# A hybrid decoder layer on one core: the last TensorE transposes of h and of the S5 table factor ea replaced by VectorE block transposes and copies through DRAM

## The chip, the cores and the metric

The kernel runs on one core of a Trainium2 chip. The metric is the device time of one execution in microseconds (us). All inputs, products and outputs are float32; the large products are made from float32 numbers split into two parts.

## The reference, cut to what matters

One decoder layer on 256 positions of width 2048. The two FFNs (width 5632) and the input and output projections of the mixer carry nearly all the work. Between the FFNs stands a mixer of two halves: an S5 state-space half (64 groups of 16 channels with 64 complex states) and a chunked gMLP half.

```python
h = h + 0.5 * swiglu(rms_norm(h, norm_ffn1), w1_gate, w1_up, w1_down)
z = rms_norm(h, norm_mix) @ w_in
y_ssm = s5_mixer(z[..., :1024], log_dt, a_re, a_im, b_re, b_im, c_re, c_im, d, w_glu)
y_gmlp = gmlp_mixer(z[..., 1024:2048], z[..., 2048:], norm_v, w_s, b_s)
h = h + concatenate([rms_norm(y_ssm, ...), rms_norm(y_gmlp, ...)]) @ w_out
h = h + 0.5 * swiglu(rms_norm(h, norm_ffn2), w2_gate, w2_up, w2_down)
gate = sigmoid(rms_norm(h, norm_ple) @ w_ple_gate)
h = h + gate * (p @ w_ple_proj)
return rms_norm(h, norm_final)

def swiglu(x, w_gate, w_up, w_down):
    return (silu(x @ w_gate) * (x @ w_up)) @ w_down
```

The S5 half depends on its inputs through tables that are functions of the parameters alone (powers of the complex step `abar`, the input factors `b`, the output factors `c`). The kernel computes these tables while FFN1 runs.

## The kernel before, in words

**The stream.** All products with large weights are one stream of steps. A group is one 512-column output of one weight; its depth is walked in steps of two 128-row slices (K slices). In a step ("tick") TensorE makes 12 matmuls of 512 columns: two slices, two halves `t` of the positions, and three products each. The weight tile `raw` is loaded by DMA on SP's queue (`L114`, 1 MB, four slices, 3 buffers), split by ScalarE (ACT) into `wh` (`L133`) and by VectorE (DVE) into the remainder `wl` (`L134`), each in 4 buffers, so the split of step i+3 is written ahead of the products of step i. The products are `wh` with the high part of the activations (`L147`), `wl` with the high part (`L148`), and `wh` with the low part (`L149`).

**The order.** The instructions stand on every engine in the order in which the Python code emits them; nothing reorders them later, and every engine works through its own row from first to last. After each step the loop adds one to `tick_no` and runs the generators that are due. A generator that yields an integer sleeps for that many ticks; under `paced` it yields costs, and sleeps one tick when their sum passes `self.budget` (0.85 in the table rounds). So `yield 6` decides after which step's instructions the next piece stands.

**h to its transpose.** The next product needs h with its columns on partitions, split in two parts: `hTh` and `hTl`, 16 slices. `h_to_T(n, gcol, flip)` makes slices 4n to 4n+3 from the finished 512-column chunk n of h. With `flip` it uses `flip()`: VectorE transposes 32x32 blocks of h into `tr` (`L367`), POOL's DMA queue stores `tr` to the DRAM buffer `gsc` (`L370`), and four DMA loads (`L373`) bring the blocks back to their partitions; after `yield 6`, ACT scales (`L232`) and copies to `hTh` (`L236`), and VectorE subtracts to `hTl` (`L238`). Without `flip`, TensorE transposes 4 blocks at a time against the identity (`L199`), twice. Chunks 0 to 2 of both FFNs and chunks 0 and 2 of `w_out` use `flip`; chunk 3 of each of these three and chunk 1 of `w_out` use TensorE. The same `flip()` also transposes the gated FFN activations (`gTa`, `gTb`, `L203`, `L204`), 22 times. There is one `tr` and two `gsc`.

**The S5 tables.** `s5_tables` runs in the first 280 us or so, in four rounds of the loop over k (`NQ` is 4). A round makes on VectorE the factor `ea` (two tiles, real and imaginary, 128x512) and others into the table tile `qt`; TensorE transposes `ea` (8 transposes of 128x128) and ACT copies them to `qt[:, 2048:3072]` (`L618`); TensorE makes 32 small products `mps` (`L623`); VectorE adds and copies these (`md`, `L628` to `L632`), and SP copies two blocks of `md` by DMA (`L634`). Then POOL sets the first column of the cosine and sine tables (`L639`, `L640`), and VectorE fills them by doubling:

```python
            g.memset(qc[:, :, 0:1], 1.0)
            g.memset(qs[:, :, 0:1], 0.0)
...
                for o, x, y, op in ((c1, c0, pc, M), (tt, s0, psn, M), (c1, c1, tt, SB),
                                    (s1, s0, pc, M), (tt, c0, psn, M), (s1, s1, tt, AD)):
                    gop(o, x, y, op)
```

In its first pass `c0` is `qc[:, :, 0:2]`, the column set by POOL and the one beside it. `put` stores parts of `qt` to DRAM on SP's queue (`L562`): columns 2048 to 4607 after `md`, columns 0 to 2047 at the end of the round.

Of the kernel before, what the change touches and what calls it, by code (L numbers as in the profile page):

```python
# [7 lines left out]
F32 = mybir.dt.float32  # L8
F32R = mybir.dt.float32r
I32 = mybir.dt.int32  # L10
AF = mybir.ActivationFunctionType
ALU = mybir.AluOpType
# [3 lines left out]
P = 128  # L16
# [5 lines left out]
NW = 512  # L22
# [32 lines left out]
class Layer:  # L55
# [166 lines left out]
        j = self.junk_p.tile([P, NW], F32, tag="junk", name="junk")  # L222
        self.nc.scalar.activation(out=j, in_=src, func=AF.Square, accum_out=acc)

    def h_to_T(self, n, gcol, flip):

        if flip:
            tr = self.flip([self.h[:, t, n * NW:(n + 1) * NW] for t in range(2)])
            yield 6
            for kk in range(4):  # L230
                v = tr.rearrange("p (i t kk u) -> p kk (i t) u", i=4, t=2, kk=4)[:, kk]
                self.nc.scalar.activation(out=v, in_=v, func=AF.Copy, scale=self.gcol[:, gcol + 4 * n + kk:gcol + 4 * n + kk + 1])  # L232
            dh, dl = (y[:, 4 * n:4 * n + 4, :].rearrange("p kk (t i u) -> p t kk i u", t=2, i=4) for y in (self.hTh, self.hTl))
            trv = tr.rearrange("p (i t kk u) -> p t kk i u", i=4, t=2, kk=4)
            for t in range(2):
                self.nc.scalar.activation(out=dh[:, t], in_=trv[:, t], func=AF.Copy)  # L236
            for t in range(2):
                self.nc.vector.tensor_tensor(out=dl[:, t], in0=trv[:, t], in1=dh[:, t].bitcast(F32), op=ALU.subtract)  # L238
            return
        for b in range(2):  # L240
            yield 1
            k0 = 4 * n + 2 * b
            ps = self.transposes(
                [self.h[:, t, (k0 + kk) * P:(k0 + kk + 1) * P] for kk in range(2) for t in range(2)])
            self.split_gain2(ps, self.gcol[:, gcol + k0:gcol + k0 + 2], self.hTh[:, k0:k0 + 2], self.hTl[:, k0:k0 + 2])

    def act_hT(self, k, t):
        return self.hTh[:, k, t * P:(t + 1) * P], self.hTl[:, k, t * P:(t + 1) * P]
# [1 line left out]
    def kernel(self):  # L250
        tc, nc, I = self.tc, self.nc, self.i
# [21 lines left out]
        self.stash = dram.tile([2 * NQ, P, BW], F32, name="stash")  # L273
        self.gsc = [dram.tile([P, 4 * 256], F32, name=f"gsc{b}") for b in range(2)]
        self.spot = 0
        self.tr = const.tile([P, 4 * 256], F32, name="tr")
        self.pools, self.cms = {}, {}

        self.plan = []
# [63 lines left out]
    def open_g(self):  # L343
        n = self.KA // 4
        self.gT_a = (self.pools["gta"].tile([P, n, 4 * 256], F32R, name="gTah"),
                     self.pools["gta"].tile([P, n, 4 * 256], F32R, name="gTal"))
        self.open("gs", "gs")

    def open_gb(self):
        self.open("gtb", "gtb")  # L350
# [9 lines left out]
    def flip(self, src):  # L360

        nc, tr = self.nc, self.tr
        trv = tr.rearrange("p (a t kk u) -> p t kk a u", a=4, t=2, kk=4)
        for t in range(2):
            nc.vector.transpose(out=trv[:, t], in_=src[t].rearrange("p (kk a u) -> p kk a u", kk=4, a=4))  # L367
        sc = self.gsc[self.spot]
        self.spot ^= 1
        nc.gpsimd.dma_start(out=sc, in_=tr)  # L370
        sv = sc.rearrange("(i f) (a x) -> a f i x", i=4, a=4)
        for a in range(4):
            nc.gpsimd.dma_start(out=tr[32 * a:32 * a + 32, :].rearrange("f (i x) -> f i x", i=4), in_=sv[a])  # L373
        return tr

    def ffn_groups(self, which):
# [42 lines left out]
        def down_post(n):  # L419
            def post(g):  # L420
                for t in range(2):
                    hs = self.h[:, t, n * NW:(n + 1) * NW]
                    self.nc.vector.scalar_tensor_tensor(
                        out=hs, in0=g.ps[t], scalar=0.5, in1=hs, op0=ALU.mult, op1=ALU.add)
                ssq = self.ssq[1 if which == 1 else 5]
                for t in range(2):
                    self.square(self.h[:, t, n * NW:(n + 1) * NW], ssq[:, n, t:t + 1])
                if n == 3:
                    self.rstd([ssq[:, i, :] for i in range(4)], D, self.r[1 if which == 1 else 4])
                yield from self.h_to_T(n, 16 if which == 1 else 48, n < 3)  # L430
            return post

        for c in range(11):
# [30 lines left out]
    def s5_tables(self):  # L464
# [20 lines left out]
        qt = T("qt", (P, QW))  # L485
# [74 lines left out]
        def put(k, lo, n, wd):  # L560
            for b in range(2):
                nc.sync.dma_start(  # L562
                    out=self.stash[2 * k + b, :, lo // 2:lo // 2 + n * wd].rearrange("p (r x) -> p r x", r=n),
                    in_=qt[:, lo:lo + 2 * n * wd].rearrange("p (r b x) -> p r b x", r=n, b=2)[:, :, b])
        self.budget = 0.85
        for k in range(NQ):
# [47 lines left out]
            yield 1  # L614
            for ri in range(2):
                ef = ea[ri].rearrange("p q t g x -> p (q t g x)")
                ps = self.transposes([ef[:, j * P:(j + 1) * P] for j in range(4)])
                nc.scalar.activation(out=qt[:, 2048 + 512 * ri:2560 + 512 * ri], in_=ps, func=AF.Copy)  # L618
            ps = self.aux_p.tile([P, NW], F32, tag="aux", name="mps")
            for q in range(8):  # L620
                o = ps[64 * (q % 2):64 * (q % 2) + 64, 32 * (q // 2):32 * (q // 2) + 32]
# [10 lines left out]
                v.tensor_copy(out=mt[s, :, 64 * a + 32:64 * a + 64], in_=md[s])  # L632
            for a in range(2):
                nc.sync.dma_start(out=mt[64 * a:64 * a + 32, :, 64 * a:64 * a + 32], in_=md[64 * a + 32:64 * a + 64])  # L634
            put(k, 2048, 5, 256)
            yield 0.6
            qc = qt[:, 0:1024].rearrange("p (q j) -> p q j", q=8)
            qs = qt[:, 1024:2048].rearrange("p (q j) -> p q j", q=8)
# [5 lines left out]
            for m in range(1, 7):  # L644
                n = 1 << m
                pc = C[:, m + 1, q0:q0 + 8].unsqueeze(2).to_broadcast([P, 8, n])
                psn = S[:, m + 1, q0:q0 + 8].unsqueeze(2).to_broadcast([P, 8, n])
                c0, s0, c1, s1 = qc[:, :, 0:n], qs[:, :, 0:n], qc[:, :, n:2 * n], qs[:, :, n:2 * n]
                tt = tmp[:, :, 0:n]
                cost = 0.1 + 0.0084 * n  # L650
                for o, x, y, op in ((c1, c0, pc, M), (tt, s0, psn, M), (c1, c1, tt, SB),
                                    (s1, s0, pc, M), (tt, c0, psn, M), (s1, s1, tt, AD)):
                    gop(o, x, y, op)
                    yield cost
            put(k, 0, 2, 512)


# [134 lines left out]
    def gmlp(self, half):  # L792
# [27 lines left out]
        self.close("gm")  # L820
        self.open("yss", "yss")
        m = self.pools["yss"]
        self.yh = m.tile([P, 8, 256], F32R, name="yh")
        self.yl = m.tile([P, 8, 256], F32R, name="yl")
        self.sg = [m.tile([P, NW], F32, name=f"sg{t}") for t in range(2)]

    def mix_groups(self):
        I, nc = self.i, self.nc
# [67 lines left out]
        def wo_post(n, rr, ssm):  # L896
            def post(g):
                for t in range(2):
                    hs = self.h[:, t, n * NW:(n + 1) * NW]
                    nc.vector.scalar_tensor_tensor(out=hs, in0=g.ps[t], scalar=rr[:, t:t + 1], in1=hs,  # L900
                                                   op0=ALU.mult, op1=ALU.add)
                if not ssm:
                    return
                for t in range(2):
                    self.square(self.h[:, t, n * NW:(n + 1) * NW], self.ssq[4][:, n, t:t + 1])
                if n == 3:
                    self.rstd([self.ssq[4][:, i, :] for i in range(4)], D, self.r[3])
                yield from self.h_to_T(n, 32, n % 2 == 0)
            return post

        def glu_post(n):
# [218 lines left out]
```

## Time and profile before

| what | value |
|---|---|
| median of 3 runs | 1851.15 us (1850.25 to 1851.33) |
| the profiled execution | 1851.49 us, its span 1849.8 us |
| TensorE (PE) busy | 1837.9 us, 99% of the span |
| VectorE (DVE) busy | 1140.3 us, 62% |
| ScalarE (ACT) busy | 854.5 us, 46% |
| GpSimd (POOL) busy | 131.0 us, 7% |
| mean granted TensorE clock | 0.998 of full speed |

The profile is one execution. PE's busy time counts pipelined matmuls whose ends are modelled, so where TensorE loses time is read from the starts of neighbouring matmuls, from its waits, and from the chain of work that ended last.

### The profile page before, as it was taken

The numbers are of one execution on the slowest core, as the hardware profiler recorded it, in microseconds if no ns is written. First come the engines' busy times: TensorE is split into PE (matmuls) and PEld (weight loads), VectorE is DVE, ScalarE is ACT, GpSimd is POOL, SyncE is SP. The second block draws the span as 40 slices with busy tenths as digits, with TensorE's granted clock in tenths as the row PEclk, the third lists the DMA queues.
The fourth block names the chain that finished last, engine by engine and source line by source line (L and its number), as shares of the span: only waits on it lengthen the run. The fifth ranks groups of instructions, "written<-read, shape, count | busy, mean of one in ns | idle before, by whom it ended". The sixth has DMA issues, their size and how long they took to land.

```text
span 1849.8 us, 21900 instructions
## 1 busy us (share of the span) xinstructions
PE 1837.9 (99%) x8512; PEld 1526.8 (83%) x8512; DVE 1140.3 (62%) x1541; ACT 854.5 (46%) x1012; POOL 131.0 (7%) x208
## 2 busy tenths in 40 slices
PE   9999999999999999999999999999999999999998
PEld 7888888888888888888888888888888888888887
DVE  6788886555545554698876555555555555455565
ACT  6444444444444444444446544444444444444454
POOL 1000000000000000022100000000000000000000
PEclk9999999999999999999999999999999999999999
DMA  8677777666656665665546666666666665566553
GB/s 324 223 244 265 235 269 253 217 217 226 220 201 216 216 216 193 225 253 210 188 163 216 213 216 217 217 226 219 222 218 217 216 216 206 204 216 216 190 204 134
DMA packets 72615, 405.10 MB, mean 219 GB/s; under 512 B 10176, under 2 KB 15552, under 8 KB 29888
## 3 DMA queue, kind: packets, MB, share of 16 engines
q1 hardware_dynamic: 62000, 371.67, 56.4%
q0 software_dynamic: 10080, 31.47, 5.8%
q8 instruction: 66, 1.08, 0.2%
q10 hardware_dynamic: 432, 0.57, 0.1%
q14 instruction: 37, 0.30, 0.0%
HBM read 376.28 MB, written 27.26 MB: 218 GB/s over the span
## 4 chain that ended last, share of the span: by engine, by line
PE 98%; DMA 1%; issue 1%; DVE 0%; ACT 0%; SPq 0%; POOLq 0%; POOL 0%; DVEq 0%; ACTq 0%
PE acc L147 32%; PE acc L149 32%; PE acc L148 32%; PE tr L199 1%; PE y L759 1%; DMA raw<-in_w_gate 1%; PE v L712 0%; PE sp L800 0%; PE mps L623 0%; PE y L753 0%; DVE wl L134 0%; ACT wh L133 0%; SPq L296 0%; DVE hg L1052 0%; DVE h L1035 0%
## 5 line engine op out<-in xcount | busy, mean ns | idle before, releaser
L134 DVE TENSOR_TENSOR wl<-raw,wh 128x1024 fp32r<-128x1024 f32 (+1 forms) x649 | 800.9, 1237 | 642.5 <-ACT wh L133 640.7
L133 ACT ACTIVATE wh<-raw 128x1024 fp32r<-128x1024 f32 (+1 forms) x649 | 685.9, 1059 | 824.3 <-PE acc L149 779.6
L147 PE MATMUL acc<-wh,hTh 128*128 128x512 f32 (+1 forms) x1744 | 680.9, 390 | 0.1
L148 PE MATMUL acc<-wl,hTh 128*128 128x512 f32 (+1 forms) x1744 | 678.1, 389 | 1.3 <-DVE wl L134 1.3
L149 PE MATMUL acc<-wh,hTl 128*128 128x512 f32 (+1 forms) x1744 | 678.2, 389 | 0.0
L148 PEld LDWEIGHTS acc<-wl,hTh 128*128 128x128 f32 x1744 | 327.5, 188 | 69.1 <-DVE wl L134 2.1
L149 PEld LDWEIGHTS acc<-wh,hTl 128*128 128x128 f32 x1744 | 327.4, 188 | 68.2
L147 PEld LDWEIGHTS acc<-wh,hTh 128*128 128x128 f32 x1744 | 327.4, 188 | 67.8 <-ACT wh L133 0.5
L147 PE MATMUL acc<-wh,gTah 128*128 128x512 f32 x384 | 149.4, 389 | 0.0
L148 PE MATMUL acc<-wl,gTah 128*128 128x512 f32 x384 | 149.4, 389 | 0.0
L149 PE MATMUL acc<-wh,gTal 128*128 128x512 f32 x384 | 149.4, 389 | 0.0
L147 PE MATMUL acc<-wh,gTbh 128*128 128x512 f32 x320 | 124.5, 389 | 0.0
L148 PE MATMUL acc<-wl,gTbh 128*128 128x512 f32 x320 | 124.5, 389 | 0.0
L149 PE MATMUL acc<-wh,gTbl 128*128 128x512 f32 x320 | 124.5, 389 | 0.0
L370 POOL DMA_DIRECT2D gsc<-tr x30 | 17.0, 568 | 1160.1 <-DVE tr L367 1160.1
L147 PEld LDWEIGHTS acc<-wh,gTah 128*128 128x128 f32 x384 | 72.1, 188 | 15.1
L148 PEld LDWEIGHTS acc<-wl,gTah 128*128 128x128 f32 x384 | 72.1, 188 | 15.0
L149 PEld LDWEIGHTS acc<-wh,gTal 128*128 128x128 f32 x384 | 72.1, 188 | 14.9
L373 POOL DMA_DIRECT2D tr<-gsc x120 | 65.5, 552 | 97.4 <-DMA gsc<-tr 91.2
L147 PEld LDWEIGHTS acc<-wh,gTbh 128*128 128x128 f32 x320 | 60.1, 188 | 12.6
L148 PEld LDWEIGHTS acc<-wl,gTbh 128*128 128x128 f32 x320 | 60.1, 188 | 12.5
L149 PEld LDWEIGHTS acc<-wh,gTbl 128*128 128x128 f32 x320 | 60.1, 188 | 12.4
(233 smaller groups left out, 1061.5 us busy)
## 6 DMA issues: line engine op xcount, KB each, us to landing
raw<-in_w_up SPq DMA_DIRECT2D x88, 1024.0 KB, 5.8
raw<-in_w_down SPq DMA_DIRECT2D x88, 1024.0 KB, 4.8
raw<-in_w_gate SPq DMA_DIRECT2D x86, 1024.0 KB, 4.8
raw<-in_w_in SPq DMA_DIRECT2D x24, 1024.0 KB, 4.8
raw<-in_w_out SPq DMA_DIRECT2D x16, 1024.0 KB, 4.8
raw<-in_w_ple_gate SPq DMA_DIRECT2D x16, 1024.0 KB, 4.9
gsc<-tr POOLq DMA_DIRECT2D x30, 512.0 KB, 3.2
tr<-gsc POOLq DMA_DIRECT2D x120, 128.0 KB, 4.4
```

What stands on the lines that cost most here:

```text
L133: nc.scalar.activation(out=wh[:, 0:nk, :], in_=src, func=AF.Copy)
L134: nc.vector.tensor_tensor(out=wl[:, 0:nk, :], in0=src, in1=wh[:, 0:nk, :].bitcast(F32), op=ALU.subtract)
L147: nc.tensor.matmul(o, ah, wh[:, j, c0:c1], start=first, stop=False)
L148: nc.tensor.matmul(o, ah, wl[:, j, c0:c1], start=False, stop=False)
L149: nc.tensor.matmul(o, al, wh[:, j, c0:c1], start=False, stop=last)
L199: self.nc.tensor.transpose(ps[:, i * P:(i + 1) * P], b, self.ident)
L370: nc.gpsimd.dma_start(out=sc, in_=tr)
L373: nc.gpsimd.dma_start(out=tr[32 * a:32 * a + 32, :].rearrange("f (i x) -> f i x", i=4), in_=sv[a])
L759: nc.tensor.matmul(ps[:, 64 * i:64 * i + 64], R[ri][:, i, :], qt[:, f0:f0 + 64], start=False, stop=(a == 1 and ri == 1))
```

## The change: what it does

1. `h_to_T` always goes through `flip()`. Chunk 3 of FFN1, of `w_out` and of FFN2, and chunk 1 of `w_out` leave TensorE. Chunk 3 sleeps 5 ticks instead of 6.
2. There are two `tr` buffers, used in turn with the two `gsc`; the second lives in pools that are open where it is needed.
3. In a table round the 8 TensorE transposes of `ea` and the two ACT copies are replaced: VectorE transposes 32x32 blocks of both halves straight into `qt`, and POOL's queue stores each half to a DRAM buffer `esc` and loads it back in 16 pieces of 32 partitions, each in runs of 32 elements.
4. The store of columns 2048 to 4607 moves to the end of the round.

```diff
-    def h_to_T(self, n, gcol, flip):
+    def h_to_T(self, n, gcol):
 
-        if flip:
-            tr = self.flip([self.h[:, t, n * NW:(n + 1) * NW] for t in range(2)])
-            yield 6
...
-        for b in range(2):
-            yield 1
-            k0 = 4 * n + 2 * b
-            ps = self.transposes(
-                [self.h[:, t, (k0 + kk) * P:(k0 + kk + 1) * P] for kk in range(2) for t in range(2)])
-            self.split_gain2(ps, self.gcol[:, gcol + k0:gcol + k0 + 2], self.hTh[:, k0:k0 + 2], self.hTl[:, k0:k0 + 2])
+        tr = self.flip([self.h[:, t, n * NW:(n + 1) * NW] for t in range(2)])
+        yield 5 if n == 3 else 6
...
-        self.tr = const.tile([P, 4 * 256], F32, name="tr")
+        self.tr = [const.tile([P, 4 * 256], F32, name="tr"), None]
+        self.esc = [dram.tile([P, NW], F32, name=f"esc{b}") for b in range(2)]
...
+        self.tr[1] = self.pools["gs"].tile([P, 4 * 256], F32, name="tr1")
...
-        nc, tr = self.nc, self.tr
+        nc, tr = self.nc, self.tr[self.spot]
...
                 ef = ea[ri].rearrange("p q t g x -> p (q t g x)")
-                ps = self.transposes([ef[:, j * P:(j + 1) * P] for j in range(4)])
-                nc.scalar.activation(out=qt[:, 2048 + 512 * ri:2560 + 512 * ri], in_=ps, func=AF.Copy)
+                et = qt[:, 2048 + 512 * ri:2560 + 512 * ri]
+                v.transpose(out=et.rearrange("p (a j u) -> p j a u", a=4, j=4),
+                            in_=ef.rearrange("p (j a u) -> p j a u", j=4, a=4))
+                g.dma_start(out=self.esc[ri], in_=et)
+                ev = self.esc[ri].rearrange("(i f) (a j u) -> a f j i u", i=4, a=4, j=4)
+                for a in range(4):
+                    for j in range(4):
+                        g.dma_start(out=qt[32 * a:32 * a + 32, 2048 + 512 * ri + P * j:2176 + 512 * ri + P * j]
+                                    .rearrange("f (i u) -> f i u", i=4), in_=ev[a, :, j])
+                yield 0.8
...
-            put(k, 2048, 5, 256)
...
+            put(k, 2048, 5, 256)
             put(k, 0, 2, 512)
...
+        self.tr[1] = m.tile([P, 4 * 256], F32, name="tr1")
```

Three places of the order of instructions show what moves. In the rows, x16 counts neighbours that read alike, and `[waits ...]` names the semaphores that an instruction waits for (`Pool`, `DVE`, `PE`, `Activation` for an engine, `DMASW` and `DMAHW` for DMAs from POOL's queue and the others).

First POOL's row in the table rounds. Before, two transfers of an FFN activation with the two memsets of round 0 behind them:

```order
L370 DMA gsc_112<-tr 128x1024
L373 DMA tr<-gsc_112 32x4x256 x4
L370 DMA gsc_113<-tr 128x1024
L373 DMA tr<-gsc_113 32x4x256 x4
L639 MEMSET qt 128x8
L640 MEMSET qt 128x8
```

The same place in the changed program:

```order
L364 DMA gsc_112<-tr 128x1024
L367 DMA tr<-gsc_112 32x4x256 x4
L364 DMA gsc_113<-tr_142 128x1024
L367 DMA tr_142<-gsc_113 32x4x256 x4
L614 DMA esc_115<-qt 128x512
L618 DMA qt<-esc_115 32x4x32 x16
L614 DMA esc_116<-qt 128x512
L618 DMA qt<-esc_116 32x4x32 x16
L640 MEMSET qt 128x8
L641 MEMSET qt 128x8
```

In each of the four rounds 34 DMA issues now stand ahead of the two memsets.

Second VectorE's row in round 1, from the second half of the new transpose (`L612`) to the first doubling step, in the changed program:

```order
L612 STREAM_TRANSPOSE qt<-ea_360 128x4x4x32 [waits DMASW3_49,DMASW4_49,DMASW2_49,DMASW1_49]
L134 TENSOR_TENSOR wl<-raw,wh 128x1024 [waits PE_49,Activation_49]
L134 TENSOR_TENSOR wl<-raw,wh 128x1024 [waits DMAHW6_49,Activation_49]
L630 TENSOR_TENSOR md<-dI,mps 128x128 [waits DMAHW1_49,DVE_49,PE_49]
L634 COPY qt<-md 64x4x32 [waits DVE_49]
L634 COPY qt<-md 64x4x32
L642 COPY qt<-C 128x8 [waits DMAHW2_49,DMAHW1_49]
L643 COPY qt<-S 128x8
L552 TENSOR_TENSOR qt<-qt,C 128x8x2 [waits DVE_49,Pool_49]
L552 TENSOR_TENSOR tmp<-qt,S 128x8x2 [waits DVE_49,Pool_49]
L552 TENSOR_TENSOR qt<-qt,tmp 128x8x2 [waits DVE_49]
L134 TENSOR_TENSOR wl<-raw,wh 128x1024 [waits Activation_49]
```

In the program before, the first doubling step carries the same wait, and only the transposes are missing:

```order
L134 TENSOR_TENSOR wl<-raw,wh 128x1024 [waits DMAHW5_49,PE_49,Activation_49]
L628 TENSOR_TENSOR md<-dI,mps 128x128 [waits DMAHW0_49,DMAHW1_49,DVE_49,PE_49]
L632 COPY qt<-md 64x4x32 [waits DVE_49]
L632 COPY qt<-md 64x4x32
L641 COPY qt<-C 128x8 [waits DMAHW1_49,DMAHW0_49]
L642 COPY qt<-S 128x8
L558 TENSOR_TENSOR qt<-qt,C 128x8x2 [waits DVE_49,Pool_49]
```

So the wait for POOL's memset is in both programs; what stands ahead of that memset on POOL is new.

Third ACT's row after the last chunk of FFN1, where the mixer's first group begins. Before, ACT's work on chunk 3 stands one and two steps after the squares of h:

```order
L223 ACTIVATE junk,ssq_102<-h 128x512 x2
L133 ACTIVATE wh<-raw 128x1024
L214 ACTIVATE hTh<-tr,gcol 128x256 x2
L133 ACTIVATE wh<-raw 128x1024
L214 ACTIVATE hTh<-tr,gcol 128x256 x2
L133 ACTIVATE wh<-raw 128x1024 x6
```

In the changed program it stands after five:

```order
L223 ACTIVATE junk,ssq_102<-h 128x512 x2
L133 ACTIVATE wh<-raw 128x1024 x5
L231 ACTIVATE tr<-tr,gcol 128x8x32 x4
L235 ACTIVATE hTh<-tr 128x4x128 x2
L133 ACTIVATE wh<-raw 128x1024 x3
```

Slices 12 to 15 of `hTh` and `hTl`, which these write, are read by TensorE in the seventh step of that group.

## Rows read from the trace of the kernel before

**Rows 1.** The page: busy time by engine, and the granted clock by slice.

```profile
PE 1837.9 (99%) x8512; PEld 1526.8 (83%) x8512; DVE 1140.3 (62%) x1541; ACT 854.5 (46%) x1012; POOL 131.0 (7%) x208
...
PEclk9999999999999999999999999999999999999999
```

**Rows 2.** The waits of PE, whole span: total us, times, longest us.

```profile
PE acc L148 <- DVE wl L134: 1.3, 2, 0.8
```

**Rows 3.** Line L199 on PE: duration ns min/median/max, first and last start.

```profile
L199 PE MATMUL tr<-ident,h x32: 270/272/273, 740.0 to 1747.3; 128*128 128x128 f32 x32
```

**Rows 4.** Timeline of PE after FFN1's last chunk: start us, us, what.

```profile
737.24 0.39 PE L147 MATMUL acc<-wh,hTh 128*128 128x512 f32 x1
...
739.96 0.60 PE L199 MATMUL tr<-ident,h 128*128 128x128 f32 x4
...
743.17 0.60 PE L199 MATMUL tr<-ident,h 128*128 128x128 f32 x4
```

**Rows 5.** The chain that ended last, table round 1: start us, us, what.

```profile
162.31 0.87 PE tr L199 x8
163.19 1.07 PE mps L623 x32
```

**Rows 6.** Timeline of POOL in table rounds: start, us, [idle before <-releaser].

```profile
101.68 0.56 POOL L370 DMA_DIRECT2D gsc<-tr  x1 [38.25 <-DVE tr L367]
105.41 2.18 POOL L373 DMA_DIRECT2D tr<-gsc  x4 [3.17 <-DMA gsc<-tr]
107.58 0.13 POOL L639 MEMSET qt<- 128x8 f32 x1
```

**Rows 7.** Timeline of DVE in table round 1.

```profile
163.00 1.22 DVE L134 TENSOR_TENSOR wl<-raw,wh 128x1024 fp32r<-128x1024 f32 x1
164.85 1.23 DVE L134 TENSOR_TENSOR wl<-raw,wh 128x1024 fp32r<-128x1024 f32 x1 [0.63 <-ACT wh L133]
...
167.07 0.18 DVE L558 TENSOR_TENSOR qt<-qt,C 128x16 f32<-128x16 f32 x1
```

**Rows 8.** DMAs of the tile md: us from issue to landing.

```profile
DMA to landing us min/median/max: 1.8/2.7/3.9
```

**Rows 9.** DMAs of the tile tr, 1010 to 1030 us (contended), issue to landing.

```profile
DMA to landing us min/median/max: 3.2/6.8/8.1
```

**Rows 10.** Timeline of PE at the start: the 32 warm-up matmuls.

```profile
1.44 6.76 PE L288 MATMUL warm<-ident 128*128 128x128 f32 x32 [1.44 <-POOL mhalf L264]
```

**Rows 11.** Timeline of DVE after FFN1's last chunk: the last step of rstd.

```profile
739.38 0.17 DVE L193 TENSOR_SCALAR rs<-rs 128x2 f32<-128x2 f32 x1
```

**Rows 12.** Timeline of one flip of chunk 0 of FFN1, on DVE, POOL and ACT.

```profile
558.63 1.29 DVE L367 STREAM_TRANSPOSE tr<-h 128x512 f32<-128x512 f32 x2
560.22 0.56 POOL L370 DMA_DIRECT2D gsc<-tr  x1 [53.67 <-DVE tr L367]
563.70 2.18 POOL L373 DMA_DIRECT2D tr<-gsc  x4 [2.92 <-DMA gsc<-tr]
572.49 1.69 ACT L232 ACTIVATE tr<-tr,gcol 128x256 f32<-128x256 f32 x4
574.87 1.29 DVE L238 TENSOR_TENSOR hTl<-tr,hTh 128x512 fp32r<-128x512 f32 x2 [1.03 <-ACT hTh L236]
```

**Rows 13.** Timeline of POOL and ACT: two flips for which ACT waited.

```profile
1286.67 0.56 POOL L370 DMA_DIRECT2D gsc<-tr  x1 [37.55 <-DVE tr L367]
1299.40 1.06 ACT L203 ACTIVATE gTah<-tr 128x1024 fp32r<-128x1024 f32 x1 [0.49 <-DMA tr<-gsc]
1330.19 0.56 POOL L370 DMA_DIRECT2D gsc<-tr  x1 [37.58 <-DVE tr L367]
1344.49 1.06 ACT L203 ACTIVATE gTbh<-tr 128x1024 fp32r<-128x1024 f32 x1 [2.06 <-DMA tr<-gsc]
```

**Rows 14.** Waits of ACT for weights, whole span; landing, 166 to 171 us.

```profile
ACT wh L133 <- DMA raw<-in_w_up: 13.9, 5, 7.3
...
stash<-qt SPq DMA_DIRECT2D x2, 640.0 KB, 4.4
```

More of the change, by code (lines that the diff above doesn't have):

```diff
@@ L223, in square @@
         self.nc.scalar.activation(out=j, in_=src, func=AF.Square, accum_out=acc)
-    def h_to_T(self, n, gcol, flip):
-        if flip:
-            tr = self.flip([self.h[:, t, n * NW:(n + 1) * NW] for t in range(2)])
-            yield 6
[L230 to L239, printed above, removed]
-        for b in range(2):
-            yield 1
-            k0 = 4 * n + 2 * b
-            ps = self.transposes(
-                [self.h[:, t, (k0 + kk) * P:(k0 + kk + 1) * P] for kk in range(2) for t in range(2)])
-            self.split_gain2(ps, self.gcol[:, gcol + k0:gcol + k0 + 2], self.hTh[:, k0:k0 + 2], self.hTl[:, k0:k0 + 2])
+    def h_to_T(self, n, gcol):
+        tr = self.flip([self.h[:, t, n * NW:(n + 1) * NW] for t in range(2)])
+        yield 5 if n == 3 else 6
+        for kk in range(4):
+            v = tr.rearrange("p (i t kk u) -> p kk (i t) u", i=4, t=2, kk=4)[:, kk]
+            self.nc.scalar.activation(out=v, in_=v, func=AF.Copy, scale=self.gcol[:, gcol + 4 * n + kk:gcol + 4 * n + kk + 1])
+        dh, dl = (y[:, 4 * n:4 * n + 4, :].rearrange("p kk (t i u) -> p t kk i u", t=2, i=4) for y in (self.hTh, self.hTl))
+        trv = tr.rearrange("p (i t kk u) -> p t kk i u", i=4, t=2, kk=4)
+        for t in range(2):
+            self.nc.scalar.activation(out=dh[:, t], in_=trv[:, t], func=AF.Copy)
+        for t in range(2):
+            self.nc.vector.tensor_tensor(out=dl[:, t], in0=trv[:, t], in1=dh[:, t].bitcast(F32), op=ALU.subtract)
     def act_hT(self, k, t):
@@ L429, in post @@
                     self.rstd([ssq[:, i, :] for i in range(4)], D, self.r[1 if which == 1 else 4])
-                yield from self.h_to_T(n, 16 if which == 1 else 48, n < 3)
+                yield from self.h_to_T(n, 16 if which == 1 else 48)
             return post
@@ L907, in post @@
                     self.rstd([self.ssq[4][:, i, :] for i in range(4)], D, self.r[3])
-                yield from self.h_to_T(n, 32, n % 2 == 0)
+                yield from self.h_to_T(n, 32)
             return post
```

## The prediction

> **What bounds the kernel now.** I read the page first: PE is busy for 1837.9 of 1849.8 us, at a granted clock of nine tenths or more in every slice [rows 1]. Then PE's waits: for the weight split it waited 1.3 us in the whole span, in two waits [rows 2]. So TensorE is fed without a gap, and only its own instruction count sets the time. Anything removed from it is gained one for one; every stall that the change gives it is lost one for one. The other engines have idle time, but it is bounded by a lead: VectorE writes the remainder `wl` three steps ahead of its use, and beyond that TensorE stands. What matters is therefore how long VectorE or ACT, which work through their rows in order, are held at one place.
>
> **What is removed.** The 32 transposes of h [rows 3] stand in eight blocks of four. A step of 12 matmuls took 739.96 - 737.24 = 2.72 us; the step with a block took 743.17 - 739.96 = 3.21 us [rows 4]. That is 0.49 us a block, 3.9 us for eight. In a table round the eight transposes of `ea` take 0.87 us of the chain, and the 32 small products follow at once, as before [rows 5]: 4 x 0.87 = 3.5 us. Together **-7.4 us**. The two ACT copies a round also go; ACT is 46% busy and nothing waits longest for it, so I count nothing.
>
> **What the tables get.** Each half of `ea` is a store on POOL's queue, then 16 loads that read what it wrote. POOL is in order: in round 0 it stored at 101.68, waited for the landing, issued its first load at 105.41, took 2.18 us for four, and the memset followed at 107.58, the moment the last issue was done [rows 6]. So an issue takes 0.545 us, and the memset cannot pass the DMAs. Now 34 issues and two landings stand ahead of it, and the first doubling step of VectorE waits for it. In round 1 of before that step ran at 167.07, five microseconds after TensorE's transposes [rows 5, 7], because the memset had long been done.
>
> Worked out for round 1, from E = 162.31, the end of the step's products [rows 5]:
> VectorE's `wl` ends at 163.00 + 1.22, so the new transposes start at E + 1.9 [rows 7] and take 1.29 as those of h do; POOL starts 0.3 later (558.63 + 1.29 to 560.22) [rows 12]: E + 3.5. From a store to its first load 563.70 - 560.22 = 3.5 us pass [rows 12]; the new store is half as large, I keep 3.5. Sixteen loads are 8.7 us. Twice 12.2 is 24.4; the memset ends at E + 28.0. Three short doubling steps (0.18 each) and the next `wl` (1.23) [rows 7] make E + 29.8. TensorE meanwhile has the small products (1.07) [rows 5], the five steps whose `wl` stands before the wait (13.6), and one matmul (0.23, a twelfth of a step): E + 14.9. It stands for 14.9 us, in four rounds 60 us. In round 3 the finished gate group's two products and their transposes also stand between the wait and the next `wl`; at 1.29 us for the transposes and as much again for the products that is 2.6 more: **+62 us**.
>
> The bounds. Below: VectorE not 1.9 us late at E, and half a microsecond less for each of the two smaller stores, gives 12.0 a round, 48 in all. Above: the program gives POOL's DMAs eight semaphores in turn, so a load waits for the one eight before it. Where a load lands in under 8 x 0.545 = 4.4 us this costs nothing. The 16 KB copies of `md`, in the same 128-byte runs, landed in 2.7 us, 3.9 at most [rows 8]; in a contended stretch the loads of `tr` had a median of 6.8 [rows 9]. With 6.8 a load would be issued every 0.85 us, 4.9 us more a set, 9.8 a round: 101 us in all. I take 0.545, because rows 8 have the same size and runs, and because a standing VectorE frees no weight buffers, so the weight loads pause.
> The Trainium skill ("DMA: Bandwidth & Descriptors", Specifications) says that pieces under 512 B are not moved at line rate, since the engine reads, changes and writes them. By that rule the loads would go towards the far end, and the sum to some 1960 instead of 1920; rows 8 show no such penalty at this size, and no row shows 32 such copies in a queue.
>
> **What the last chunk of h gets.** Its transfer stands after the row statistics: VectorE is done with them at 739.38 + 0.17 [rows 11], so the transposes end at 740.84 and the store starts 0.3 later. Against G = 737.24, the start of the next group [rows 4], that is G + 3.9. Where ACT waited for a transfer, the data was there 1299.40 - 1286.67 = 12.7 us after the store, elsewhere 14.3 [rows 13]. From ACT's start to the end of the last subtraction 574.87 + 1.29 - 572.49 = 3.7 us pass [rows 12]. TensorE uses the last of it in the sixth matmul of the seventh step, 6 x 2.72 + 5 x 0.227 = G + 17.4. So ACT may start at G + 13.8, and with 12.7 it starts at G + 16.6: 2.8 us late, 4.5 with 14.3. Below, with 3.5 us to the first load, 1.6 to the fourth and 3.2 for its landing [rows 9, 12], the data is there at G + 12.2, in time. I take 2.8, since the weight loads run in this stretch as beside rows 13. Three such places (after FFN1, after `w_out`, after FFN2): **+8 us**, from 0 to 13. What is late there is ACT, and behind it the next splits; their lead of three steps covers 3 us. Chunk 1 of `w_out` sleeps 6 ticks, with a group of 4 ticks and more behind it before its slices are read: nothing.
>
> **The clock.** No row of before shows a TensorE that stood for long. The nearest row is the warm-up at the start: 32 matmuls took 6.76 us [rows 10], where 8 of the same shape take 0.87 later [rows 5], so 3.3 us were lost after idleness, though the granted clock reads full. Four stalls of some 15 us may each cost 0 to 3.3; I take the middle, **+6 us**.
> The Trainium skill ("TensorE: Matmul & The Clock Gate", Part 1) says that an idle TensorE falls to half its clock and gets it back through activity. By it each stall pays in full and the sum would be 1926 instead of 1920; no row of before shows the fall.
>
> **The stores at the end of a round.** Two of 640 KB (4.4 us to land) now go out with the two others, ahead of weight loads on SP. ACT waited for `w_up` five times in the span, 13.9 us, 7.3 at most [rows 14], and TensorE never felt it. I count 0; if all of the 4.4 us came on top where that lead is used up, it would be 18 us in four rounds. The second `tr` only takes away a wait of the next transfer for the last: 0.
>
> **The sum.** 1851.5 (the profiled execution, 0.3 above the median of the runs) - 7.4 + 62 + 8 + 6 = 1920 us; 0.3 is nothing beside the bounds.
>
> **The rivals.**
> *All of it is hidden: faster.* VectorE's wait at the memset stays inside the lead, and ACT's start is in time at chunk 3. From `wl` of one step to its need there are about 6 us of lead, so this needs the memset by about E + 13, with POOL through 34 issues in 10 us, 0.3 each. For it: nothing shown; against it: 0.545 in every group of four. It gives 1851.5 - 7.4 = 1844. It would also come if the doubling's wait were met by an earlier memset, which the order does not show.
> *The tables are hidden, the last chunks are late: no change.* 1851.5 - 7.4 + 8 = 1852.
> *POOL's loads crawl.* Landings of 6.8 us or more, and the late stores' 18 us beside: 1920 + 39 to 1920 + 57, so 1959 to 1977. For it: 64 KB a load set in 2048 short pieces; against it: rows 8.
> *The clock falls at each stall.* 1926, and inside the main case.
>
> **Chances.** The main case, VectorE held by the memset with loads at POOL's pace, 0.77; its own bounds are 1851.5 - 7.4 + 48 = 1892 and, with 62, 13 and 13 for the three terms and 18 for the stores, 1950. Crawling loads 0.12; no change 0.05; faster 0.06. A kernel of this spread tells 0.2%, 3.7 us, from no change. So faster 0.06, same 0.05, slower 0.89. A range from 1890 to 1960 leaves out the two cases near or below 1852 and most of the crawl, under 2 in 10.
>
> **What would show it.** In the profile after: PE waits for `wl` L134 four times, 12 to 17 us each, between 110 and 330 us; VectorE's longest waits are at the first doubling step, released by POOL's memset, some 20 us each; POOL's row shows 16 loads at 0.55 each behind each store. Three further waits of PE of 2 to 4 us at the seventh step after the last chunks, released by ACT or VectorE's `hTl`. No TensorE transposes of `ea` or h. The forecast is wrong if VectorE's wait at the memset is below 8 us, or if POOL issues or lands the short loads at another pace than 0.55 us.

## The result

The changed kernel took 1944.59 us (median of 4 runs, 1942.26 to 1946.1) against 1851.24 us (1850.25 to 1852.02) for the kernel before beside it: ratio 1.0505, 95% interval 1.0492 to 1.0519, so 5% slower. That lies in the forecast's range and on the forecast's side, 25 us above the forecast itself. The profiled execution took 1942.26 us, its span is 1940.5 us: 90.7 more than before.

The page of the changed kernel, which answers to [rows 1]:

```profile
PE 1844.2 (95%) x8448; PEld 1527.2 (79%) x8448; DVE 1143.4 (59%) x1549; ACT 854.2 (44%) x1012; POOL 216.4 (11%) x364
...
PEclk9989889799999999999999999999999999999999
```

The waits of PE and of DVE, whole span (total us, times, longest us), which answer to [rows 2]:

```profile
PE acc L148 <- DVE wl L134: 68.1, 6, 17.9
PE acc L147 <- ACT hTh L235: 14.9, 3, 7.4
...
DVE qt L552 <- POOL qt L641: 90.2, 4, 24.4
```

TensorE has 64 instructions fewer and stands for 83 us at these two lines, where it stood for 1.3. Almost all of it is seven waits: four for `wl` in the table rounds (15.32, 16.10, 17.90 and 17.77 us, 67.1 together) and three for `hTh` at the last chunks of h (1.61, 5.88, 7.44: 14.9). VectorE's four long waits are for POOL's memset.

Timeline of POOL, DVE and PE in table round 0 (start us, us, what, [idle before <-releaser]); it answers to [rows 6, 7].

```profile
112.15 0.56 POOL L614 DMA_DIRECT2D esc<-qt  x1 [5.98 <-DVE qt L612]
117.42 4.87 POOL L618 DMA_DIRECT2D qt<-esc  x9 [4.71 <-DMA esc<-qt]
123.47 3.79 POOL L618 DMA_DIRECT2D qt<-esc  x7 [1.18 <-DMA qt<-esc]
127.25 0.56 POOL L614 DMA_DIRECT2D esc<-qt  x1
129.86 8.66 POOL L618 DMA_DIRECT2D qt<-esc  x16 [2.05 <-DMA esc<-qt]
138.51 0.13 POOL L640 MEMSET qt<- 128x8 f32 x1
...
138.68 0.18 DVE L552 TENSOR_TENSOR qt<-qt,C 128x16 f32<-128x16 f32 x1 [21.90 <-POOL qt L641]
...
139.06 1.22 DVE L134 TENSOR_TENSOR wl<-raw,wh 128x1024 fp32r<-128x1024 f32 x1
...
140.34 0.80 PE L148 MATMUL acc<-wl,hTh 128*128 128x512 f32 x1 [15.32 <-DVE wl L134]
```

Read it downwards: store, landing, 16 loads at 8.66/16 = 0.54 us, store, landing, 16 loads; only then the memset, then three short VectorE steps, then the `wl` for which TensorE stands. From the first store to the memset 26.4 us pass; in round 1 it is 25.0 (185.05 to 210.06).

The granted clock behind this stall, in stretches of 1 us (busy us and instructions of PE, PEld, DVE, ACT, POOL; clock; DMA share; GB/s). Before, it was 1.00 over the whole stretch from 100 to 345 us.

```profile
124.00:125.00 1.00, 1.00 (x5) 0.52 (x3) 0.00 (x0) 0.17 (x1) 1.00 (x3) 1.00 0.07 16
128.00:129.00 1.00, 0.00 (x0) 0.00 (x0) 0.00 (x0) 0.00 (x0) 0.00 (x0) 0.50 0.76 262
140.00:141.00 1.00, 0.66 (x2) 0.57 (x3) 0.93 (x7) 0.00 (x0) 0.00 (x0) 0.50 0.00 0
144.00:145.00 1.00, 1.00 (x4) 0.81 (x3) 0.97 (x4) 0.00 (x0) 0.00 (x0) 0.50 0.63 238
145.00:146.00 1.00, 1.00 (x5) 0.83 (x5) 0.97 (x4) 0.68 (x1) 0.00 (x0) 0.99 1.01 426
```

TensorE stops at 125.0. At 128 the clock is at its half level (1.2 of 2.4 GHz), and it stays there for the first 4.7 us of work after 140.34, in which a matmul starts every 0.43 us instead of every 0.23: eleven took 4.78 us (140.34 to 145.12) where they otherwise take 2.49.

The timeline of FFN2's last chunk in the changed kernel, on DVE, POOL, SP and ACT:

```profile
1820.29 1.28 DVE L417 SCALAR_TENSOR_TENSOR h<-acc,h 128x512 f32<-128x512 f32 x2
...
1822.79 1.30 DVE L361 STREAM_TRANSPOSE tr<-h 128x512 f32<-128x512 f32 x2
...
1824.64 0.60 POOL L364 DMA_DIRECT2D gsc<-tr  x1 [0.96 <-ACT wh L133]
1829.25 2.19 POOL L367 DMA_DIRECT2D tr<-gsc  x4 [4.01 <-DMA gsc<-tr]
...
1825.22 3.67 SPq L114 DMA_DIRECT2D raw<-in_w_ple_proj  x2
1828.94 0.42 SPq L977 DMA_DIRECT2D pTr<-in_pT  x1
1829.41 0.42 SPq L979 DMA_DIRECT2D gfb<-in_gfb  x1
...
1842.07 1.70 ACT L231 ACTIVATE tr<-tr,gcol 128x256 f32<-128x256 f32 x4 [9.36 <-DMA tr<-gsc]
```

The DMA view of the same stretch, 1824 to 1843 us (issues, KB each, median us to landing):

```profile
gfb<-in_gfb SPq DMA_DIRECT2D x1, 1024.0 KB, 11.5
...
tr<-gsc POOLq DMA_DIRECT2D x4, 128.0 KB, 10.1
```

The four loads of `tr` (1829.25 to 1830.88) go out in the same microsecond in which SP issues its second weight load (1828.56), `pTr` and `gfb`, and take 10.1 us. From store to ACT's start it is 17.4 us here, 14.9 after `w_out`, 11.6 after FFN1 (the forecast took 12.7 from [rows 13]).

### The profile page after: what moved, and what is told of

It is laid out like the page before. It is cut to its first block, busy times and chain, and to the rows that moved or that the text cites. A ratio compares the mean times of both kernels' runs of the same rounds, so it can differ in the third digit from the quotient of the medians.

```text
span 1940.5 us, 21974 instructions
## 1 busy us (share of the span) xinstructions
PE 1844.2 (95%) x8448; PEld 1527.2 (79%) x8448; DVE 1143.4 (59%) x1549; ACT 854.2 (44%) x1012; POOL 216.4 (11%) x364
## 5 line engine op out<-in xcount | busy, mean ns | idle before, releaser
L147 PE MATMUL acc<-wh,hTh 128*128 128x512 f32 (+1 forms) x1744 | 685.4, 393 | 15.2 <-ACT hTh L235 14.9
L367 POOL DMA_DIRECT2D tr<-gsc x136 | 74.2, 552 | 117.4 <-DMA gsc<-tr 93.0
L147 PEld LDWEIGHTS acc<-wh,gTah 128*128 128x128 f32 x384 | 72.1, 188 | 14.9
L149 PEld LDWEIGHTS acc<-wh,gTal 128*128 128x128 f32 x384 | 72.1, 188 | 14.9
L618 POOL DMA_DIRECT2D qt<-esc x128 | 69.3, 549 | 31.0 <-DMA esc<-qt 20.9
```

Of the source, the lines that this page charges most:

```text
L147: nc.tensor.matmul(o, ah, wh[:, j, c0:c1], start=first, stop=False)
L149: nc.tensor.matmul(o, al, wh[:, j, c0:c1], start=False, stop=last)
L618: g.dma_start(out=qt[32 * a:32 * a + 32, 2048 + 512 * ri + P * j:2176 + 512 * ri + P * j] .rearrange("f (i u) -> f i u", i=4), in_=ev[a, : ...
```

## The experiments

Theory from the forecast: the tables cost because POOL, in order, holds the memset and with it VectorE behind 34 DMA issues; the last chunks cost because their transfer is late; the clock adds a little. Rivals: short loads that land slowly; a last chunk whose cost is contention rather than the late start; a slow clock that comes from something other than the standing.

**The two parts apart.** h alone (tables as before), and tables alone (h as before).

> The h part of the change alone: all chunks of h through VectorE and DRAM with two buffers, the tables and their stores as in the kernel before. Theory (the parts add up): no wait for wl of more than 1 us, the three waits for the last chunk of h as in the profile after (1.6, 5.9, 7.4 us), half clock after the two long ones (some 2.5 us each), and 3.9 us of transposes gone: 1851 - 4 + 15 + 5 = 1867 us. Rival (the last chunks are late only because the table part has shifted the weight loads): within 3 us of 1847.

> The table part alone, with two buffers: ea through VectorE and DRAM and the stores at the round's end, the chunks of h as in the kernel before. Theory: four waits for wl of 15 to 18 us and four stretches at half clock, 3.5 us of transposes gone, no wait for the last chunk of h: 1851 - 3.5 + 67 + 11 = 1925 us. If the two parts do not add up to the changed kernel's 1944.6 (e2 and e3 together 93 us over 1851), they share a cost.

Measured: h alone 1866.03 us, 1.0082 [1.0066, 1.0099], with two waits for `hTh` (3.69 after FFN1, 4.71 after FFN2, none after `w_out`). The four runs of h alone go from 1861.31 to 1868.78 us and the profile is of the fastest, so these two waits are its smallest share. Tables alone 1924.21 us, 1.0399 [1.0381, 1.0416], four waits of 15.3 to 17.3 us. 15.9 + 74.1 = 90 of the 93 us: the parts add up to within 3 us.

**The memset ahead of the DMAs**, in the whole change and in the tables alone:

```diff
+            g.memset(qc[:, :, 0:1], 1.0)
+            g.memset(qs[:, :, 0:1], 0.0)
             for ri in range(2):
                 ef = ea[ri].rearrange("p q t g x -> p (q t g x)")
...
-            g.memset(qc[:, :, 0:1], 1.0)
-            g.memset(qs[:, :, 0:1], 0.0)
```

> The changed kernel with POOL's two memsets of the first table column written ahead of the 34 DMA issues of the round. Theory (VectorE is held by a memset that stands behind POOL's DMA issues): TensorE's four waits for wl of 15 to 18 us (67 us in the profile after) go, and with them four stretches at half clock; what stays of them is a flip of a finished FFN chunk that now queues behind the 34 issues, in rounds 2 and 3, some 15 us; three waits for the last chunk of h stay (15 us). So 1875 to 1892 us. Rival (the new transposes on VectorE, the short copies beside the weight loads, or the stores at the round's end hold the weight split): the waits stay at 50 us or more and the time above 1920.

> The table part alone with the memsets ahead of the DMA issues. Theory: no wait for the memset; the finished FFN chunks queue behind the 34 issues on POOL in rounds 2 and 3, which costs up to 15 us; 3.5 us of transposes gone: 1848 to 1866 us. If POOL's queue does not delay them (a flip has slack of about 6 us on ACT's side), 1848. Rival (the short copies or the stores themselves hold the split): above 1880.

Measured: 1899.4 us, 1.0268 [1.0252, 1.0283], and 1882.66 us, 1.0179 [1.0164, 1.0194]. VectorE no longer waits for POOL, which gives back 45 and 42 us. But both are slower than expected: the second victim behind the same queue, for which the expectations had up to 15 us in two rounds, cost waits of 21.8 and 23.8 us, nearly all of them in three, with slow work behind them. PE's waits in the tables alone with the memset first:

```profile
PE acc L147 <- ACT wh L133: 23.8, 4, 9.9
```

The timeline of POOL and ACT ahead of the fourth of them, in the same kernel:

```profile
315.89 8.66 POOL L630 DMA_DIRECT2D qt<-esc  x16 [5.00 <-DMA esc<-qt]
324.54 0.56 POOL L372 DMA_DIRECT2D gsc<-tr  x1
...
332.82 1.06 ACT L203 ACTIVATE gTah<-tr 128x1024 fp32r<-128x1024 f32 x1 [17.63 <-DMA tr<-gsc]
```

The chunk's own transfer (`gsc`, for `gTah`) is issued right behind the last of the 32 loads. ACT waits 17.63 us for it, splits no weights meanwhile, and TensorE stands 9.9 us.

**Fewer issues.** Tables alone, memset first, 4 loads with 512-byte runs a half instead of 16 with 128-byte runs; two ACT copies at the round's end make the order that the 16 loads made.

```diff
-                    for j in range(4):
-                        g.dma_start(out=qt[32 * a:32 * a + 32, 2048 + 512 * ri + P * j:2176 + 512 * ri + P * j]
-                                    .rearrange("f (i u) -> f i u", i=4), in_=ev[a, :, j])
+                    g.dma_start(out=et[32 * a:32 * a + 32].rearrange("f (i x) -> f i x", i=4), in_=ev[a])
```

> The part on the tables alone, h as before, memsets ahead of the transfers, and each half of ea fetched by 4 loads with 512-byte runs in place of 16 with 128-byte runs; the order inside a row that the 16 loads made is made by two ACT copies at the round's end. POOL has 10 issues a round ahead of what follows instead of 34. With 34 and the memset first the time was 1882.7 us, and the transfers of the FFN chunks queued behind them. Theory (the cost is POOL's queue: 0.55 us an issue and a wait for each landing): POOL is held 2 x 3.5 + 10 x 0.55, some 12.5 us a round instead of 26 to 36, the chunk's transfer is inside its lead of six ticks, and only the transposes removed from TensorE remain: before less 3.5, 1847 us (1845 to 1850), PE waits for wh under 1 us. Rival (the landing waits and contention, not the number of issues): the ACT waits for the chunks' transfers shrink by a third at most and 1865 or more remains.

Measured: 1849.33 us, 0.9994 [0.9985, 1.0003]. No PE wait in the table rounds is over 0.4 us. POOL in round 3:

```profile
270.34 0.56 POOL L626 DMA_DIRECT2D esc<-qt  x1 [11.99 <-DVE qt L624]
274.27 2.17 POOL L629 DMA_DIRECT2D qt<-esc  x4 [3.38 <-DMA esc<-qt]
276.43 0.56 POOL L626 DMA_DIRECT2D esc<-qt  x1
281.31 2.17 POOL L629 DMA_DIRECT2D qt<-esc  x4 [4.31 <-issue]
283.47 0.56 POOL L372 DMA_DIRECT2D gsc<-tr  x1
```

13.1 us instead of some 26. From 34 issues to 10 a round 33 us went, though the transfers of `esc` landed no faster (median 4.4 us, against 2.0 in the changed kernel, whose weight loads pause in the stalls). The pieces grew with the same edit (128 to 512 bytes), but an issue took 0.54 us with either, and what POOL's rows lost is the time of 24 issues, 13 us a round: the number of issues is the cost. The short tables with the memset left in its old place were not run. The last matmul starts 3.54 us earlier than before (1836.88 against 1840.42), just what the transposes were worth, but the span is only 1.8 us shorter; more on that below.

**The row statistics behind the transposes.** In `h_to_T` the flip of chunk 3 is issued first, then `rstd` (`stat` in the diff), then comes the yield; with h alone, and in the whole change.

```diff
-                if n == 3:
-                    self.rstd([ssq[:, i, :] for i in range(4)], D, self.r[1 if which == 1 else 4])
-                yield from self.h_to_T(n, 16 if which == 1 else 48)
+                yield from self.h_to_T(n, 16 if which == 1 else 48, stat)
```

> The part on h alone, with the row statistics of the last chunk behind its transposes instead of ahead of them (the same sums, later). The part alone took 1866.0 us, with TensorE waits of 3.7 and 4.7 us at two of the three last chunks. Theory (ACT's start is late by the length of the transfer, which starts late behind the statistics): VectorE's transposes start some 1.3 us earlier, the store and the loads with them, and each of the two waits is shorter by about 1.3 us: 1863 us. Rival (what sets the landing is which 1 MB weight load is under way when the four loads are issued): the waits do not follow the earlier store, they stay or jump by several us in either direction, 1862 to 1872 us.

> The whole change with the row statistics of the three last chunks behind their transposes, all else as the change has it. In the changed kernel TensorE waited 1.6, 5.9 and 7.4 us at these places, 14.9 together, with some 2.7 us of slow clock behind the two longer ones. Theory (the transfer starts 2.3 us too late, and late enough to fall together with the next 1 MB weight load): the transfers start 2.3 us earlier and land 2 to 4 us faster, the waits fall to a third, 1944.6 - 10 - 5 = 1929 us (1925 to 1934). Rival (only the start counts): each wait falls by 2.3 us, 1944.6 - 1.6 - 2.3 - 2.3 = 1938.

Measured: h alone 1850.41 us, 1.0001 [0.9993, 1.001], where 1866 stood: faster than both the theory (1863) and the rival (1862 to 1872) had it. The whole change 1924.15 us, 1.04 [1.0386, 1.0414], where 1944.6 stood, a microsecond below the theory's range. All three waits of 14.9 us together are gone from the whole change. The timeline of FFN2's last chunk there, on DVE, POOL and SP:

```profile
1811.62 1.28 DVE L418 SCALAR_TENSOR_TENSOR h<-acc,h 128x512 f32<-128x512 f32 x2
1812.82 1.29 DVE L362 STREAM_TRANSPOSE tr<-h 128x512 f32<-128x512 f32 x2
...
1814.66 0.56 POOL L365 DMA_DIRECT2D gsc<-tr  x1 [54.26 <-ACT junk L223]
1818.03 2.19 POOL L368 DMA_DIRECT2D tr<-gsc  x4 [2.81 <-DMA gsc<-tr]
...
1816.05 4.17 SPq L114 DMA_DIRECT2D raw<-in_w_ple_proj  x2
1820.27 0.43 SPq L976 DMA_DIRECT2D pTr<-in_pT  x1
1820.75 0.42 SPq L978 DMA_DIRECT2D gfb<-in_gfb  x1
```

The DMA view of 1814 to 1825 us of the same kernel:

```profile
tr<-gsc POOLq DMA_DIRECT2D x4, 128.0 KB, 3.8
```

Counted from the update of h, the transposes start 1.3 us earlier (1.20 against 2.50), the store 1.3, the loads 2.6 (6.41 against 8.96) and ACT 9.4 (12.43 against 21.78). The expectation's 2.3 us for the earlier start was thus too much, and the rival by which only the start counts is out: most of the gain at this place is that the loads land in 3.8 us instead of 10.1, now that they go ahead of the second weight load, `pTr` and `gfb`.

No run moved the weight loads alone, but h alone without the mending comes near to it: after `w_out` the statistics stand ahead of the transposes as in the change, while the second weight load is issued at 1037.58, behind all four loads of `tr` (1034.90 to 1036.53). The DMA view of 1030 to 1046 us there:

```profile
tr<-gsc POOLq DMA_DIRECT2D x4, 128.0 KB, 3.4
```

No wait follows. Being ahead of that load is not the whole account, though: in the mended h part the loads at the same place took 7.4 to 7.7 us with the next weight load behind them, and TensorE still waited 2.23 us.

**Idle work in the stalls.** The whole change, with matmuls that nothing reads ahead of the four steps that wait; first 60 at each, then 74, 73, 81 and 69.

```diff
+            if i in (43, 62, 81, 100):
+                idle = self.aux_p.tile([P, NW], F32, tag="aux", name="idle")
+                for _ in range(60):
+                    nc.tensor.matmul(idle, g.act(k0, 0)[0], split[i][0][:, 0, :], start=True, stop=True)
```

> The whole change, with 60 matmuls of 128x512 that nothing reads added to TensorE at each of the four table stalls, ahead of the step that waits (13.6 us of work in a stall of 15.3 to 17.9). Theory (a stall also costs some 2.7 us behind it, because TensorE restarts at half clock): the work stands inside the wait, the granted clock is full when the wait ends, and the time falls by 4 x 2.7, to some 1934 us, though TensorE has 240 matmuls more. Rival (the slow matmuls behind a stall come from late weights or a throttle that the idle time does not set): the time stays at 1944 or rises by up to 4 x 13.6 to 1999.

> The whole change with 74, 73, 81 and 69 idle matmuls at the four table stalls instead of 60 each, so that less than a microsecond of each stall is left. With 60 each, TensorE still stood 4.1, 3.7, 5.4 and 2.6 us, the granted clock still fell to 0.50 behind three of the four, and some 7 us of the 10.8 were still lost in the slow steps behind them (2.65 + 1.6 + 2.7 + 0); the time had fallen by 3.9 to 1940.75 us. Theory (the fall needs only that TensorE stands for some microseconds, and costs some 2.7 us whatever the stall's length): now the granted clock stays full through all four and the time falls by 7 more, to 1934 us (1931 to 1937), though TensorE has 297 matmuls more than the changed kernel. Rival (the half clock comes from what follows the stall, not from the standing): 1940 or more, as with 60.

Measured: 1940.75 us, 1.048 [1.0465, 1.0494], and 1945.92 us, 1.0515 [1.0501, 1.053]. The stretches behind the first stall with 60, where TensorE still stood 4.05 us (the clock is the third number from the end):

```profile
143.00:144.00 1.00, 0.86 (x2) 0.77 (x3) 0.93 (x9) 0.00 (x0) 0.00 (x0) 0.50 0.00 0
146.00:147.00 1.00, 1.00 (x4) 0.81 (x3) 1.00 (x3) 0.00 (x0) 0.00 (x0) 0.50 0.65 131
```

The same stretch with 74, where it stood 0.37 us:

```profile
143.00:144.00 1.00, 0.63 (x4) 0.21 (x3) 0.98 (x3) 0.00 (x0) 0.00 (x0) 1.00 0.00 0
```

With the full set the clock stayed at 1.00 behind the first three stalls (stands of 0.37, 1.10 and 0.66 us) and fell to 0.50 for some 3 us behind the fourth (2.10). So the clock does follow from the standing. By the starts of the 30 matmuls behind each stall, slow work cost 2.30, 2.36, 1.57 and 2.79 us in the changed kernel and 0.15, 0.13, 0.14 and 1.74 with the full set, 6.9 us less. But the time did not come back as my theory had it: the rival's number, 1940 or more, is what came. The stalls themselves grew: idle work (0.227 us a matmul) and remaining wait together are 70.2 us with 60 and 71.6 with the full set, against 67.1. In round 0 POOL's second store landed later, with waits of 4.25 and 3.63 us ahead of its first load instead of 2.05. And with the full set TensorE, now fast behind the stalls, stood another 3.4 us for `wh` and `wl` in later steps (1.14, 0.95, 0.76 and 0.51), which it did not in the changed kernel. So 7.9 us of longer stalls and other waits stand against the 6.9. Why the store lands later stays open. Both profiles are of the slowest of their four runs (1934.29 to 1941.87 and 1942.49 to 1948.62 us), so this account is of those executions.

**Put together.** Two mended versions: the short tables with only chunk 1 of `w_out` from the h part, and everything off TensorE with both mendings.

> The kernel of the short tables (4 loads a half, memsets first) and, of h, only chunk 1 of w_out as the change has it, the three last chunks by TensorE as before. Theory (what the change costs is POOL's queue in the tables and the late transfer of the three last chunks, and nothing else of it costs): before less 3.5 for the tables' transposes and 0.98 for two blocks of h, 1850.1 - 4.5 = 1845.6 us, no PE wait over 1 us. Rival (chunk 1 of w_out is late as well, or the second transpose buffer costs something): 1848 to 1855, with a wait for hTh near 1050 us.

> All 64 transposes off TensorE as in the change, but with the short tables (4 loads a half with 512-byte runs, memsets first, two ACT copies at the round's end) and the row statistics behind the last chunks' transposes. By the two parts apart (1850.4 for h with the statistics behind, 1849.3 for the short tables, 1850.8 before) the sum is 1849 us, 1846 to 1852: the 7.4 us taken from TensorE are given back in some 2 us of a wait at w_out's last chunk with its slow clock and some 2 us at the program's end. If w_out's wait falls away as well, 1845.

Measured: 1849.22 us, 0.9995 [0.9986, 1.0004], and 1851.84 us, 1.0012 [1.0003, 1.0021]. The first came 3.6 us above its theory, at the rival's number but without the rival's wait near 1050 us: its last matmul starts 3.25 us earlier than before (1837.17), and 2.2 us of that are lost behind it. In the second PE waits for no more than 0.9 us at a time behind its warm-up, and its last matmul ends 4.7 us earlier than before, yet the kernel is no faster. Its 11 runs go from 1850.07 to 1857.15 us and the profiled one took 1850.21, so what made the others longer no row shows. The last one is the mended h part without `w_out`'s last chunk:

> The part on h alone with the row statistics behind the transposes, and w_out's last chunk left to TensorE as before, so that six of its eight blocks are off TensorE and the place where the mended h part still waited (2.2 us, with a slow clock behind it) is gone. Theory: 6 x 0.49 us taken from TensorE, against two waits of 0.5 and 0.6 us for the split of p that the mended h part showed behind FFN2: before less 2.9 plus 1.1, 1848.7 us (1847 to 1850.5), no wait for hTh over 1 us. Rival (the waits at the other two places come back, since the weight loads stand otherwise): 1851 to 1856.

Measured: 1848.45 us, 0.999 [0.9981, 0.9999]: the two waits at `p` and none for `hTh`, as expected. It is the only one of the 12 experiments whose interval lies below 1, by 2.0 us, 0.1%, and its upper end is only just below.

## Why the prediction was right

The forecast was 1920 us; its steps, against the profiled execution (1942.26, 22 us more):

- **What is removed, -7.4.** Right in the instruction count (64 fewer); the two experiments without waits bear out the size: 3.5 forecast and 3.54 measured at the last matmul for the tables, 2.9 less 1.2 of new waits, so 1.7, against 1.74 there (1838.68 against 1840.42) for six blocks of h.
- **POOL holds VectorE, +62.** Right in place, releaser and size: 67.1 us. A round's chain from the first store to the memset was forecast at 24.4 us and took 26.4, 25.0, 27.8 and 25.5; the waits at the memset were 21.7 to 24.4 (some 20 forecast), and the price of an issue is 0.54. Moving the memset removed these waits, so this is shown. What the step did not see is that the chunks' transfers queue behind the same issues; it mattered only once the memset was gone from the queue.
- **Crawling loads.** Out: the transfers of `esc` landed in 1.8 to 5.5 us, median 2.0. In five of the eight sets POOL waited between the first loads and the next (1.18 us above; 6.5 us in all, which are inside the 67.1). The Trainium skill ("DMA: Bandwidth & Descriptors", Specifications) has pieces under 512 B move below line rate. Whether that or the weight loads beside them made these landings late no row here separates. A set is 256 KB, not the 64 KB that the forecast writes in its rival.
- **The last chunks, +8.** The place and the way (ACT late at the seventh step) were right, the size was not: 14.9 us, with 0 to 13 as bounds. The step took 12.7 us from store to ACT; it was 11.6, 14.9 and 17.4, and with these the forecast's own sum gives 1.7, 5.0 and 7.5 against the measured 1.61, 5.88 and 7.44. The failing assumption is that the weight loads run here as beside [rows 13], so that one time fits all three places: the loads of `tr` took 5.9 us after FFN1, 7.2 after `w_out` and 10.1 after FFN2 (medians), and after FFN2 a weight load, `pTr` and `gfb` were issued within 0.7 us of the first of them.
- **The clock, +6.** Mis-sized. From the span's 90.7 us take 67.1 + 14.9 - 7.4 = 74.6 and 2.5 at the program's end: 13.6 us are left, 2.3 for each of six stalls (four of the tables, two of the last chunks). The starts of the matmuls bear it out: 9.0 us behind the four, 2.35 and 2.00 behind the two, and 0.41 behind the wait of 1.61. The forecast had 1.5 for each of four, between 0 and 3.3 (four times 3.3 makes 1927 in full, not its 1926), and nothing behind the last chunks. It agrees with the statistics experiment: the span fell by 16.1 us for 14.9 of waits although waits for `wl` and `p` grew by 3.4, so 4.6 for two. By rows the clock read 0.50 for 4.7 us of work behind the first stall, 3.1 to 5.7 behind the six. The forecast found no row of before that shows the fall; there is one, behind the last matmul (it is shown in the last section). The Trainium skill ("TensorE: Matmul & The Clock Gate", Part 1) has an idle TensorE fall to half its clock and regain it by working; the rows of this case agree (1.00 at 125 us, 0.50 from 128, 1.00 again from 145). Filling the table stalls took 6.9 of the 9.0 us away, but other waits came in their place, some of them for the weight splits; how much of the 13.6 a clock that stays full would save is not settled.
- **The stores, 0.** Right for TensorE: no wait of PE for ACT's `wh` is over 0.2 us in the changed kernel. Chunk 1 of `w_out`, 0: right, no wait for `hTh` stands there in any of the runs.
- **Not in the forecast:** 2.5 us at the program's end.

So 5 + 7 + 8 + 2.5 us explain the 22.

## What to carry to other kernels

Before moving work to a DMA queue of an in-order engine, list what else is issued on that engine behind it and multiply the issues by their price: here the queue, not the bytes, cost 67 us, and moving the memset ahead and cutting 34 issues to 10 removed the waits. A transfer on a deadline is priced at the place where it runs, with the loads that are issued in the same microseconds: after FFN2 1.3 us of earlier start bought 9 us of earlier arrival. And 7 us off a saturated engine are soon eaten: in the mended whole by waits of under 1 us each and by 3.4 us more behind the last matmul.

## What the runs showed that was not expected

TensorE's clock falls after short stands too: with 60 idle matmuls it read 0.50 behind 4.05 us as it did behind 15; behind 2.56 us it stayed at 1.00 there, and behind 2.10 us in the full set it read 0.50 for some 3 us. In the tables alone with the memset first it read 0.50 for some 3 us behind two stands of only 1.10 and 0.76 us, 1.3 us apart, and in the full set it stayed at 1.00 behind 1.14 and 0.95, 1.5 us apart: the length of a stand alone does not order these cases. The fall can be seen in the kernel before too, at its end, where the last matmul starts at 1840.42 (columns as above):

```profile
1843.00:1844.00 1.00, 0.00 (x0) 0.00 (x0) 0.32 (x2) 0.17 (x1) 0.55 (x1) 0.98 0.00 0
1844.00:1845.00 1.00, 0.00 (x0) 0.00 (x0) 1.00 (x3) 0.55 (x1) 0.00 (x0) 0.50 0.00 0
```

The program's end differs between programs. The DMA view of the last 10 us of the kernel before (GB/s in slices of 0.25 us):

```profile
GB/s 0 0 0 0 0 0 0 0 0 0 0 0 0 0 0 0 0 0 0 0 0 164 401 393 369 393 352 377 377 377 402 385 205 0 0 0 0 0 0 0
```

The same view for everything moved with both mendings:

```profile
GB/s 0 0 0 0 0 0 0 8 328 393 385 393 385 369 401 377 385 393 344 33 0 0 0 0 0 0 0 0 0 0 0 0 0 0 0 0 0 0 0 0
```

Behind the last byte of the output 1.75 us pass before, 5.0 there; 4.25 in the changed kernel and in all four experiments that keep both its parts and its 34 issues, 2.75 with the tables alone, 3.5 with the short tables, 1.75 and 1.5 with h alone. No row of work stands in that time. In the profiled executions it took 1.8 of the 3.5 us that the short tables gained and 3.3 of the 4.7 that everything mended gained, and what causes it is open: the number of DMA issues does not order the values.
